# Four lo buffers, activation pairs used in turns, and overwritten TensorE products at the start and between the blocks

## The chip, the cores and the metric

The kernel runs on one core of one Trainium2 chip. The metric is the device time of one execution in microseconds (us), lower is better; the median of the runs is compared. The engines are named as the profile names them: PE is TensorE, with PEld for its weight loads, DVE is VectorE, ACT is ScalarE, POOL is GpSimd, and SP is the engine that issues the DMAs of the weights.

## What is computed

Two different transformer blocks, each two layers deep, run one after the other on one sequence of 256 tokens of width 1024, in fp32. Cut to what matters:

```python
def first_block(x, c, ...):            # 2 layers
    c_act = silu(c)
    for l in range(DEPTH):
        sh1, sc1, gt1, sh2, sc2, gt2 = split(c_act @ w_ada[l] + b_ada[l], 6)
        y = mixer(x * (1 + sc1) + sh1, ...)          # attention and a 31-tap convolution, gated, @ w_out
        x = layer_norm(DN_ALPHA * x + (1 + gt1) * y, ...)
        h = square(relu((x * (1 + sc2) + sh2) @ w_up[l])) @ w_down[l]
        x = layer_norm(DN_ALPHA * x + (1 + gt2) * h, ...)
def second_block(x, ...):              # 2 layers
    for l in range(DEPTH):
        h = rmsnorm(x, ln_mix_g[l])                  # three attentions, gated and merged, @ w_o
        x = x + merged @ w_o[l]
        h = rmsnorm(x, ln_ffn_g[l])
        x = x + (silu(h @ w_ffn_gate[l]) * (h @ w_ffn_up[l])) @ w_ffn_down[l]
    return rmsnorm(x, final_norm_g)
```

So the program is a row of eight stages: mixer and feed-forward of the first block, twice, and the same of the second block, twice.

## The kernel before, in words

**Products.** PE multiplies fp32 operands as sums of three products of a shorter type: each operand is split into a high part (hi) and a remainder (lo), and PE forms hi·hi, hi·lo and lo·hi. Activations are kept as such pairs in SBUF (`u`, and `s`, `mg`, `n_` from `new_fm`).

**Weights.** `fetch()` (L120 to L140) takes the next weight tile of 1 MB: SP's DMA brings it into `raw` (3 buffers), ACT casts it into `whi` (L138, two halves, 4 buffers), DVE subtracts `raw - whi` into `wlo` (L139, two halves, 3 buffers). `w(ahead)` fetches so that one to three tiles are under way before they are used. PE reads `whi` and `wlo` in a few helpers: `ws2` (L175 hi, L177 lo) for the up weights of the feed-forward, `as_` (L206, L207 with lo, L208), and `as_512` (L222, L223 with lo, and L228) for the first piece of a stage. A `wlo` buffer comes free when PE has done its last product from it; until then the DVE subtraction that will fill it again stands and waits, with all that is queued behind it on DVE.

**Order.** PE's order is the order in the code (`manual_schedule` on PE). The orders of DVE and ACT are set by a scheduler at build time, except inside `handover`, where they stand as written too. The scheduler places a cast or a subtraction where it expects its buffers to be free, so the number of buffers changes the order.

**Handovers.** `handover` (L676) joins two stages: the last products of a stage (`out.tail`, with L206 to L208), the normalisation on DVE (`front` and `stats`, for the first block L761 to L778, for the second L841 to L883), eight transposes on PE per half of the tokens (`transposed`, L732), the new hi and lo activations (`finish`, ACT L796 and L801 or L907, DVE L794 and L803 or L905), and the first products of the next stage (`as_512`, L222, L223, L228). The tokens are worked on in two halves of 128, so that each handover has a first and a second set of transposes. There are seven between stages and one at the end. The fourth, between the blocks, is the long one: it has a layer norm and an RMS norm in a row (`ln_rms`).

**Feed-forward of the first block.** Up weights (`ws2`, L175 and L177) and down weights (`add`, L206 to L208) alternate. The up result is evacuated by ACT (L188) and DVE (L189), squared by ACT (L1118, L1119) and split by ACT (L150) and DVE (L151). Between them DVE also does row products for later layers (`ada_dot`, L374) and gates (L419, L421, after the small PE product L418, a 128x128 by 128x256 product in fp32).

**Memory.** Beside `raw`, `whi` and `wlo`, a pool `s8` of four 8 KB buffers holds activations, and `u2` has one pair of 16 KB for `u`.

Of the kernel before, what the change touches and what calls it, by code (L numbers as in the profile page):

```python
# [9 lines left out]
F32 = mybir.dt.float32  # L10
F32R = mybir.dt.float32r
# [5 lines left out]
P = 128  # L17
D = 1024
S = 256
KT = D // P  # L20
# [44 lines left out]
class Net:  # L65
    def __init__(self, ctx, tc, ins, out, stop=None, dump=None):
        self.tc, self.nc, self.i, self.out = tc, tc.nc, ins, out
        self.stop, self.dumps = stop, dump or {}
        self.uid = 0
        self.pools = {}  # L70
        for name, bufs in (("raw", 3), ("whi", 4), ("wlo", 3), ("s8", 4), ("u2", 1), ("s4", 7), ("b4", 2), ("one", 1), ("sm", 3)):
            self.pool(ctx, name, bufs)
        self.pool(ctx, "ps", 8, space=PSUM)
        self.pool(ctx, "dr", 1, space=bass.MemoryType.DRAM)
        self.queue = weight_order(ins)
        self.ready = []
        self.tracks = []
        self.behind = []
        self.ada = {}

# [152 lines left out]
    class Out:  # L233
# [27 lines left out]
        def tail(self, h, *parts):  # L261
            for part in parts:
                for p in self.last:
                    self.emit(p, h, part)


    def rstd(self, v, w):

# [78 lines left out]

    def new_u(self):

        t = self.t("u2", [P, 2, KT, S], F32R)  # L350
        return t[:, 0], t[:, 1], t

    def new_fm(self, n=KT, pool="s8"):
        return self.t(pool, [P, n, S], F32R), self.t(pool, [P, n, S], F32R)

    def par_(self, name, at, n=1):
# [173 lines left out]
    def start(self):  # L530
# [11 lines left out]
        a, n = PC["b_ada"]  # L542
        self.par1 = self.t("one", [P, n], tag="par1")
        nc.vector.tensor_scalar(self.par1, self.par[:, a:a + n], 1.0, None, op0=ALU.add)
        u = self.new_u()
        xT = self.t("s8", [P, KT, S])
        A, B = self.ada_cols(0, 1), self.ada_cols(0, 0)
        ps = [self.ps() for _ in range(8)]
        self.con = self.t("one", [P, NCC], tag="con")
        self.ident = self.con[:, 0:P]  # L550
        a, n = CC["cmask"]
        self.cmask = self.con[:, a:a + n]
        self.x = self.t("one", [P, 2, D], tag="x")
        for k in range(KT):
# [17 lines left out]
            for m in range(4):  # L572
                o = ps[6 + m // 2][:, (m % 2) * S:(m % 2) * S + S]
                b = slice((12 + m) * P, (13 + m) * P)
# [88 lines left out]
    def handover(self, out, ch, nxt=None):  # L663


        res = []
        E = mybir.EngineType
        with self.tc.manual_schedule(engines={E.PE, E.DVE, E.Activation}):
            out.tail(0, *PARTS)
            for _ in ch.front(0):  # L670
                pass
            fill = ch.front(1)
            out.tail(1, *PARTS[:2])
            if ch.ln_rms:
                out.tail(1, PARTS[2])
            ch.stats(0, itertools.islice(fill, 2))  # L676
            ch.transposed(0)
            if not ch.ln_rms:
                out.tail(1, PARTS[2])
            if ch.ln_rms or not ch.u:  # L680
                for _ in fill:
                    pass
            fin = ch.finish(0, fill)
            next(fin)
            g = nxt(ch.u) if nxt else None
            if g:
                next(g)
            for _ in fill:
                pass
            ch.stats(1, fin if ch.ln_rms else ())  # L690
            ch.transposed(1)
            last = [*fin]
            if g:
                res.append(next(g))
            last = [*ch.finish(1)][-1]
            if g:
                res.append(next(g))
        self.behind = [i.ins for i in last]
        self.after = ch.after()
        return res  # L700
# [8 lines left out]
    class Norm:  # L709
# [11 lines left out]
            lo, hi = PARTS[n]  # L721
            return slice(lo, hi), self.acc[h][lo // 512][:, lo % 512:lo % 512 + hi - lo]

        def transposed(self, h):

            net = self.net
            if not self.u:
                return
            ps = [net.ps().rearrange("p (k t) -> p k t", k=4) for _ in range(2)]
            at = self.tr[h] = lambda k, n=1: ps[k // 2 % 2][:, k // 4 * 2 + k % 2:k // 4 * 2 + k % 2 + n, :]  # L730
            for k in range(KT):
                self.nc.tensor.transpose(at(k)[:, 0, :], self.y[h][:, k * P:(k + 1) * P], net.ident)  # L732
# [257 lines left out]
    def mixer1(self, l, u, ps):  # L990
# [58 lines left out]
        def qkf(h):  # L1049
            r = slice(64 * (h % 2), 64 * (h % 2) + 64)  # L1050
            return qT[r, h // 2, :], kT[r, h // 2, :]
        gt = [self.t("s8", [P, KT, S]) for _ in range(2)]

        def gates(b, cs):
            for c in cs:
# [38 lines left out]
        gates(1, [3])  # L1094
        self.finish(ada)
        self.dump(f"hc{l}", hc[0].bitcast(F32))
        mg = self.new_fm()

        def merge(s):
            nc.vector.tensor_add(gt[0][:, s, :], gt[0][:, s, :], gt[1][:, s, :])  # L1100
# [108 lines left out]
    def mixer2(self, l, u, ps):  # L1209
# [1 line left out]
        gq = self.row(i["mla_g"][l])  # L1211

        pcs = [[p for _, p in ps], [p for _, p in self.as_512(u)]]
        n_ = self.new_fm()
        mn = self.mla_norm(pcs, gq, n_)
        next(mn)
        wkr = self.w()
# [4 lines left out]
        p = self.ps()  # L1222
# [43 lines left out]
        for h in range(2):  # L1266
# [3 lines left out]
            for n in range(2):  # L1270
                p = self.ps()
# [5 lines left out]
            kcs.append(kc)  # L1277
        next(gka)
        qTc = self.t("s8x", [P, 8, S])
        kTc = self.t("s8", [P, 8, S])  # L1280
        for src, dst in ((qcs, qTc), (kcs, kTc)):
            for h in range(2):
                tok = slice(h * P, (h + 1) * P)
# [37 lines left out]
            self.dump(f"yb{l}", y[0].bitcast(F32))  # L1321
        ab = self.track(rest(), 22, 62)

        gt = [self.t("s8x" if b == 1 else "s8", [P, KT, S]) for b in range(3)]
        bh = self.small(24, "bgh")
        nc.vector.tensor_scalar(bh, self.par_("b_gate", l * 24, 24), 0.5, None, op0=ALU.mult)
        for b in (2, 0, 1):
            for c in range(4):
                w = self.w()
                for m in range(2):  # L1330
                    k = 2 * c + m
# [1 line left out]
                    nc.scalar.copy(g, p[:, S:])  # L1333
                    nc.vector.tensor_add(g, p[:, :S], g)
                    nc.scalar.activation(g, g, AF.Tanh, scale=0.5, bias=bh[:, b * 8 + k:b * 8 + k + 1])
        mg = self.new_fm()
        for b in (2, 0, 1):
            if b == 1:
                self.finish(ab)
# [156 lines left out]
def build(tc, ins, out, stop=None, dump=None):  # L1496
    with ExitStack() as ctx:
# [5 lines left out]
            net.block1()  # L1503
        if stop is None or stop.startswith("2"):
            with ExitStack() as c2:
                for name, bufs in (("bias", 3), ("s8x", 1)):
                    net.pool(c2, name, bufs)
                net.block2()
        net.dump("x", net.x)
# [148 lines left out]
```

## Time and profile before

| | us |
|---|---|
| median of 3 runs | 1733.07 |
| lowest, highest | 1732.88, 1734.87 |
| the profiled execution | 1733.14 |
| its span in the trace | 1731.2 |
| PE busy in the span | 1661.8 (96%) |
| DVE busy in the span | 1281.8 (74%) |
| ACT busy in the span | 958.8 (55%) |

The profiled execution took 1733.14 us, of which the trace covers 1731.2 us; 1.94 us lie around the span. It is 0.07 us from the median of the runs. The granted TensorE clock was 0.989 of full speed over the span.

A row of a chain or of a timeline reads: start in us from the span's start, duration in us, engine, line, what it does. In square brackets stands how long the engine sat idle before it and whose work ended that idle time. `x8` at the end means that eight like instructions are shown as one row. PE's products are pipelined, so that one product's row overlaps with the next: the time between two starts is what a product costs.

### The profile page before, as it was taken

The numbers are of one execution on the slowest core, as the hardware profiler recorded it, in microseconds if no ns is written. First come the engines' busy times: TensorE is split into PE (matmuls) and PEld (weight loads), VectorE is DVE, ScalarE is ACT, GpSimd is POOL, SyncE is SP. The second block draws the span as 40 slices with busy tenths as digits, with TensorE's granted clock in tenths as the row PEclk, the third lists the DMA queues.
The fourth block names the chain that finished last, engine by engine and source line by source line (L and its number), as shares of the span: only waits on it lengthen the run. The fifth ranks groups of instructions, "written<-read, shape, count | busy, mean of one in ns | idle before, by whom it ended". The sixth has DMA issues, their size and how long they took to land.

```text
span 1731.2 us, 25828 instructions
## 1 busy us (share of the span) xinstructions
PE 1661.8 (96%) x10008; PEld 1436.9 (83%) x10008; DVE 1281.8 (74%) x2497; ACT 958.8 (55%) x1750; POOL 2.6 (0%) x12
## 2 busy tenths in 40 slices
PE   6998999998999999997999999999999999999998
PEld 5887888787888888885988898888889888988887
DVE  7999788578997886557856677766676566876665
ACT  3564375464355375553566754655455677455553
POOL 0000000000000000000000000000000000000000
PEclk9999999999999999998999999999999999999999
DMA  8884568584874466653544444555545444445551
GB/s 337 342 318 173 199 223 316 196 294 176 308 247 182 171 229 233 219 192 140 208 152 150 147 151 179 195 195 195 191 150 203 149 147 146 164 168 198 182 190 72
DMA packets 59974, 347.37 MB, mean 201 GB/s; under 512 B 6558, under 2 KB 10700, under 8 KB 25676
## 3 DMA queue, kind: packets, MB, share of 16 engines
q1 hardware_dynamic: 59852, 345.73, 55.3%
q8 instruction: 78, 1.28, 0.3%
q14 instruction: 44, 0.36, 0.1%
HBM read 344.63 MB, written 2.64 MB: 201 GB/s over the span
## 4 chain that ended last, share of the span: by engine, by line
PE 89%; DVE 7%; DMA 2%; ACT 1%; issue 0%; SPq 0%; DVEq 0%; ACTq 0%
PE ps L175 23%; PE ps L177 12%; PE ps L207 8%; PE ps L206 8%; PE ps L208 8%; PE ps L160 5%; PE ps L161 5%; PE ps L164 4%; PE ps L228 3%; PE ps L222 3%; PE ps L223 2%; DVE wlo L139 2%; PE ps L439 1%; PE ps L332 1%; PE ps L487 1%; PE ps L464 1%
## 5 line engine op out<-in xcount | busy, mean ns | idle before, releaser
L139 DVE TENSOR_TENSOR wlo<-raw,whi 128x1024 fp32r<-128x1024 f32 (+1 forms) x534 | 629.7, 1211 | 206.3 <-PE ps L177 104.0
L138 ACT CAST whi<-raw 128x1024 fp32r<-128x1024 f32 (+1 forms) x534 | 534.1, 1043 | 279.4 <-PE ps L208 80.6
L175 PE MATMUL ps<-u,whi 128*128 128x512 f32 x1728 | 438.9, 396 | 0.0
L175 PEld LDWEIGHTS ps<-u,whi 128*128 128x128 f32 x1728 | 313.9, 188 | 65.3 <-issue 5.7
L206 PE MATMUL ps<-whi,s 128*128 128x512 f32 (+2 forms) x688 | 253.6, 369 | 3.8 <-ACT whi L138 3.8
L207 PE MATMUL ps<-wlo,s 128*128 128x512 f32 (+2 forms) x688 | 253.0, 368 | 0.5 <-DVE wlo L139 0.5
L208 PE MATMUL ps<-whi,s 128*128 128x512 f32 (+2 forms) x688 | 252.3, 367 | 0.0
L177 PEld LDWEIGHTS ps<-u,wlo 128*128 128x128 f32 x1728 | 235.6, 190 | 17.2
L177 PE MATMUL ps<-u,wlo 128*128 128x256 f32 x1728 | 240.7, 282 | 0.0
L206 PEld LDWEIGHTS ps<-whi,s 128*128 128x128 f32 x688 | 130.3, 189 | 23.9 <-ACT whi L138 4.0
L208 PEld LDWEIGHTS ps<-whi,s 128*128 128x128 f32 x688 | 130.0, 189 | 21.0 <-DVE s L151 0.7
L207 PEld LDWEIGHTS ps<-wlo,s 128*128 128x128 f32 x688 | 130.2, 189 | 19.8 <-DVE wlo L139 1.2
L222 PE MATMUL ps<-whi,u 128*128 128x512 f32 x240 | 98.2, 409 | 11.0 <-ACT u L801 10.9
L188 ACT COPY ev<-ps 128x256 f32<-128x256 f32 x136 | 50.2, 369 | 92.1 <-PE ps L177 92.1
L952 DVE SCALAR_TENSOR_TENSOR s<-s,dw,s 128x255 f32<-128x255 f32 (+17 forms) x240 | 96.2, 462 | 0.0
L223 PE MATMUL ps<-wlo,u 128*128 128x512 f32 x240 | 96.0, 400 | 0.0
L160 PE MATMUL ps<-u,whi 128*128 128x256 f32 x352 | 89.4, 292 | 0.2 <-DVE s L941 0.2
L161 PE MATMUL ps<-u,whi 128*128 128x256 f32 x352 | 85.9, 282 | 0.0
L160 PE MATMUL ps<-s,whi 128*128 128x256 f32 x320 | 82.4, 289 | 0.0
L161 PE MATMUL ps<-s,whi 128*128 128x256 f32 x320 | 81.0, 285 | 0.3 <-DVE s L151 0.3
L189 DVE TENSOR_TENSOR ev<-ps,ev 128x256 f32<-128x256 f32 x136 | 56.8, 420 | 28.9 <-ACT ev L188 28.1
L151 DVE TENSOR_TENSOR s<-ev,s 128x256 fp32r<-128x256 f32 (+1 forms) x72 | 39.1, 542 | 48.9 <-PE ps L207 37.7
(263 smaller groups left out, 2123.2 us busy)
## 6 DMA issues: line engine op xcount, KB each, us to landing
raw<-in_w_fgu_dram SPq DMA_DIRECT2D x44, 1024.0 KB, 4.8
raw<-in_w_up_dram SPq DMA_DIRECT2D x32, 1024.0 KB, 5.0
raw<-in_w_down_dram SPq DMA_DIRECT2D x32, 1024.0 KB, 5.6
raw<-in_w_in_dram SPq DMA_DIRECT2D x32, 1024.0 KB, 4.8
ada<-in_w_ada_p_dram SPq DMA_DIRECT2D x48, 512.0 KB, 5.1
raw<-in_w_gate_dram SPq DMA_DIRECT2D x24, 1024.0 KB, 4.8
raw<-in_w_fd_dram SPq DMA_DIRECT2D x22, 1024.0 KB, 4.8
raw<-in_w_in_b_dram SPq DMA_DIRECT2D x18, 1024.0 KB, 6.1
```

The source lines that it names most:

```text
L138: nc.scalar.copy(hi[:, a:b], raw[:, a:b])
L139: nc.vector.tensor_sub(lo[:, a:b], raw[:, a:b], hi[:, a:b].bitcast(F32))
L160: mm(ps, whi[:, b], ahi[:, k, :], start=j == 0, stop=False)
L161: mm(ps, whi[:, b], alo[:, k, :], start=False, stop=False)
L175: mm(p2, whi[:, (blk + k) * P:(blk + k + 1) * P], both[:, :, k, :], start=k == 0, stop=False)
L177: mm(p[:, :S], wlo[:, (blk + k) * P:(blk + k + 1) * P], uhi[:, k, :], start=False, stop=k == KT - 1)
L206: mm(ps, ahi[:, k, tok], whi[:, cols], start=first, stop=False, **grp)
L207: mm(ps, ahi[:, k, tok], wlo[:, cols], start=False, stop=False, **grp)
L208: mm(ps, alo[:, k, tok], whi[:, cols], start=False, stop=last, **grp)
L222: mm(p, ahi[:, k, tok], whi[:, cols], start=k == 0, stop=False)
L223: mm(p, ahi[:, k, tok], wlo[:, cols], start=False, stop=False)
L952: nc.vector.scalar_tensor_tensor(cv[:, ct, d:], hp[:, ct, :S - d], wk, cv[:, ct, d:], op0=ALU.mult, op1=ALU.add)
```

## The change

It has four parts.

- `wlo` has 4 buffers where it had 3.
- The pool `s8` is gone. The pool `u2` holds two tags, `ua` and `ub`, of one 16 KB pair each, and `new_u` takes them in turns. What lived in `s8` (`xT`, the gates `gt`, the merged pair `mg`, the normed pair `n_`) now lives in `ua`, `ub` or the pool `s8x`, which has 2 buffers where it had 1.
- `warm(p, src, n)` writes n products of 128x128 by 128x256 in fp32 into a PSUM tile that the next products overwrite. `start` does 6 of them from `c_row`, which is ready early, ahead of its first product.
- `transposed` does 12 of them from the constants `con` ahead of the first and 8 ahead of the second set of transposes, in the handover between the blocks only.

```diff
-        for name, bufs in (("raw", 3), ("whi", 4), ("wlo", 3), ("s8", 4), ("u2", 1), ("s4", 7), ("b4", 2), ("one", 1), ("sm", 3)):
+        for name, bufs in (("raw", 3), ("whi", 4), ("wlo", 4), ("u2", 1), ("s4", 7), ("b4", 2), ("one", 1), ("sm", 3)):
...
+        self.turn = False
...
+    def warm(self, p, src, n):
+        for _ in range(n):
+            self.nc.tensor.matmul(p[:, :256], src[:, :P], src[:, :256], start=True, stop=True)
...
     def new_u(self):
-        t = self.t("u2", [P, 2, KT, S], F32R)
+        self.turn = not self.turn
+        t = self.pair("ua" if self.turn else "ub", F32R)
         return t[:, 0], t[:, 1], t
-    def new_fm(self, n=KT, pool="s8"):
+    def pair(self, tag, dt=F32):
+        return self.t("u2", [P, 2, KT, S], dt, tag=tag)
+
+    def new_fm(self, n, pool):
...
-        xT = self.t("s8", [P, KT, S])
+        xT = self.pair("ub")[:, 0]
...
         ps = [self.ps() for _ in range(8)]
+        self.warm(ps[0], self.c_row[:, 0:512], 6)
...
-            ch.transposed(0)
+            ch.transposed(0, 12 if ch.ln_rms else 0)
...
-            ch.transposed(1)
+            ch.transposed(1, 8 if ch.ln_rms else 0)
...
-        def transposed(self, h):
+        def transposed(self, h, warm=0):
...
             ps = [net.ps().rearrange("p (k t) -> p k t", k=4) for _ in range(2)]
+            net.warm(ps[0].rearrange("p k t -> p (k t)"), net.con, warm)
...
-        gt = [self.t("s8", [P, KT, S]) for _ in range(2)]
+        gt = self.pair("ub")
+        gt = [gt[:, b] for b in range(2)]
...
-        mg = self.new_fm()
+        mg = self.pair("ua", F32R)
+        mg = mg[:, 0], mg[:, 1]
...
-        n_ = self.new_fm()
+        n_ = self.pair("ub", F32R)
+        n_ = n_[:, 0], n_[:, 1]
...
-        kTc = self.t("s8", [P, 8, S])
+        kTc = self.t("s8x", [P, 8, S])
...
-        gt = [self.t("s8x" if b == 1 else "s8", [P, KT, S]) for b in range(3)]
+        gt = self.pair("ub")
+        gt = [gt[:, 0], self.t("s8x", [P, KT, S]), gt[:, 1]]
...
-                for name, bufs in (("bias", 3), ("s8x", 1)):
+                for name, bufs in (("bias", 3), ("s8x", 2)):
```

The order in which the instructions stand on the engines changes with it. Line numbers of the changed kernel are higher: its L139 and L140 are L138 and L139 of before, L151 and L152 are L150 and L151, L386 is L374, L809 is L794.

DVE in the first handover (mixer to feed-forward), from the residual sum of the second half (L765) on. `wlo` is the lo part of a weight, `x` the residual, `bn` the sums for the norm, `ev` and `u` the activations on their way to PE. Before:

```order
L765 SCALAR_TENSOR_TENSOR x_119<-x_119,ev_2287 128x512
L768 BN_STATS bn_346_2286<-x_119 128x6
L139 TENSOR_TENSOR wlo_2151<-raw_2148,whi_2150 128x1024 x2
L794 TENSOR_SCALAR ev_2284<-ps_2262,pl_a_2161,pl_b_2162 128x128 x2
L768 BN_STATS bn_346_2286<-x_119 128x6
```

The same place in the changed kernel:

```order
L780 SCALAR_TENSOR_TENSOR x_122<-x_122,ev_2288 128x512
L783 BN_STATS bn_344_2287<-x_122 128x6
L809 TENSOR_SCALAR ev_2285<-ps_2263,pl_a_2162,pl_b_2163 128x128 x2
L783 BN_STATS bn_344_2287<-x_122 128x6
L776 TENSOR_TENSOR ev_2298<-ps_2076,G_262_1685 128x256
```

The subtraction for the weight no longer stands between the norm and the activations; it is done before the handover begins. The same pair of subtractions has left the middle of all seven handovers between stages.

ACT in the first feed-forward, around the casts of three weights (`whi_3229`, `whi_3268` and `whi_3329` before; `whi_3230`, `whi_3269` and `whi_3330` in the changed kernel). Before:

```order
L150 CAST s_486_3127<-ev_3083 128x512
L188 COPY ev_3174<-ps_3175 128x256
L188 COPY ev_3174<-ps_3202 128x256
L150 CAST s_501_3223<-ev_3174 128x512
...
L150 CAST s_517_3323<-ev_3274 128x512
L138 CAST whi_3229<-raw_3227 128x1024 x2
L138 CAST whi_3268<-raw_3266 128x1024 x2
L138 CAST whi_3329<-raw_3327 128x1024 x2
```

In the changed kernel:

```order
L151 CAST s_484_3128<-ev_3084 128x512
L139 CAST whi_3230<-raw_3228 128x1024 x2
L189 COPY ev_3175<-ps_3176 128x256
L189 COPY ev_3175<-ps_3203 128x256
...
L151 CAST s_515_3324<-ev_3275 128x512
L139 CAST whi_3269<-raw_3267 128x1024 x2
L139 CAST whi_3330<-raw_3328 128x1024 x2
```

The first of the three casts has moved two up results ahead, the other two stay where they were.

DVE at the same place, from the last evacuation (L189, L190) of the up result on; `ada` is a row product for a later layer, `G` a gate, `s` the split up result. Before:

```order
L189 TENSOR_TENSOR ev_3274<-ps_3302,ev_3274 128x256
L139 TENSOR_TENSOR wlo_3230<-raw_3227,whi_3229 128x1024 x2
L374 ISA ada_3263,ada_515_3298<-ada_3263,c_row_95,par_98 128x1024
L374 ISA ada_515_3298 128x1
L139 TENSOR_TENSOR wlo_3269<-raw_3266,whi_3268 128x1024 x2
L374 ISA ada_3296,ada_515_3298<-ada_3296,c_row_95,par_98 128x1024
L374 ISA ada_515_3298 128x1
L151 TENSOR_TENSOR s_518_3324<-ev_3274,s_517_3323 128x512
L419 TENSOR_TENSOR G_497_3192<-ps_3359,b_447_2881 128x256
```

In the changed kernel:

```order
L190 TENSOR_TENSOR ev_3275<-ps_3303,ev_3275 128x256
L152 TENSOR_TENSOR s_516_3325<-ev_3275,s_515_3324 128x512
L431 TENSOR_TENSOR G_495_3193<-ps_3360,b_445_2882 128x256
L433 TENSOR_SCALAR G_495_3193<-G_495_3193 128x256
L386 ISA ada_3264,ada_513_3299<-ada_3264,c_row_92,par_95 128x1024
L386 ISA ada_513_3299 128x1
L140 TENSOR_TENSOR wlo_3270<-raw_3267,whi_3269 128x1024 x2
```

The subtraction of the first weight is gone from here (it is done earlier), and that of the second, which stood ahead of the split sum `s`, now stands behind it, two gate instructions and a row product.

## Rows read from the trace of the kernel before

**Rows 1.** The page: busy time and share by engine, and the chain that ended last

```profile
PE 1661.8 (96%) x10008; PEld 1436.9 (83%) x10008; DVE 1281.8 (74%) x2497; ACT 958.8 (55%) x1750; POOL 2.6 (0%) x12
...
PE 89%; DVE 7%; DMA 2%; ACT 1%; issue 0%; SPq 0%; DVEq 0%; ACTq 0%
```

**Rows 2.** PE's waits: line, for whom, us in total, times, longest us

```profile
PE ps L732 <- DVE s L883: 18.0, 8, 8.3
...
PE ps L967 <- DVE s L952: 5.8, 1, 5.8
```

**Rows 3.** Timeline of the first handover: start, us, engine, line, [idle before, releaser]

```profile
210.64 2.36 DVE L139 TENSOR_TENSOR wlo<-raw,whi 128x1024 fp32r<-128x1024 f32 x2
...
214.40 0.50 PE L222 MATMUL ps<-whi,u 128*128 128x512 f32 x1 [3.02 <-ACT u L801]
...
219.02 0.54 DVE L778 TENSOR_SCALAR x<-x,mv,r_r 128x512 f32<-128x512 f32 x1
...
220.67 1.04 PE L732 MATMUL ps<-con,x 128*128 128x128 f32 x8
```

**Rows 4.** Two stretches of 2 us: busy time by engine, PEclk, DMA share, GB/s

```profile
216.00:218.00 2.00, 2.00 (x6) 1.58 (x5) 1.79 (x8) 0.41 (x1) 0.00 (x0) 0.50 0.56 234
...
806.00:808.00 2.00, 2.00 (x6) 1.52 (x5) 1.42 (x5) 2.00 (x5) 0.29 (x1) 0.50 0.97 314
```

**Rows 5.** Timeline of PE in the second handover

```profile
411.03 0.50 PE L222 MATMUL ps<-whi,u 128*128 128x512 f32 x1 [3.02 <-ACT u L801]
...
416.34 0.85 PE L732 MATMUL ps<-con,x 128*128 128x128 f32 x6 [0.48 <-DVE x L778]
```

**Rows 6.** The chain of waits in the second handover: start, us, what

```profile
407.27 2.36 DVE wlo L139 x2
```

**Rows 7.** The chain of waits in the fourth handover

```profile
783.44 2.35 DVE wlo L139 x2
```

**Rows 8.** Timeline of PE in the fourth handover

```profile
792.43 1.94 PE L732 MATMUL ps<-con,s 128*128 128x128 f32 x8 [8.28 <-DVE s L883]
...
804.61 1.25 PE L732 MATMUL ps<-con,s 128*128 128x128 f32 x8 [3.44 <-DVE s L883]
```

**Rows 9.** Timeline of the fifth handover

```profile
1073.23 2.36 DVE L139 TENSOR_TENSOR wlo<-raw,whi 128x1024 fp32r<-128x1024 f32 x2 [1.25 <-PE ps L207]
...
1078.65 0.39 PE L223 MATMUL ps<-wlo,u 128*128 128x512 f32 x1
...
1080.79 1.06 PE L732 MATMUL ps<-con,s 128*128 128x128 f32 x8 [1.75 <-DVE s L883]
```

**Rows 10.** Timeline of the first feed-forward, two down weights and the next up weight

```profile
320.26 0.40 PE L206 MATMUL ps<-whi,s 128*128 128x512 f32 x1
...
325.73 0.59 PE L418 MATMUL ps<-b,ones 128*128 128x256 f32 x2
...
325.97 2.19 PE L175 MATMUL ps<-u,whi 128*128 128x512 f32 x8
...
335.08 5.78 ACT L138 CAST whi<-raw 128x1024 fp32r<-128x1024 f32 x6
...
336.18 0.80 PE L206 MATMUL ps<-whi,s 128*128 128x512 f32 x1 [3.84 <-ACT whi L138]
...
338.43 1.28 DVE L374 CUSTOM_DVE_ANT_0 ada<-ada,c_row,par 128x1024 f32<-128x1024 f32 x1
...
344.47 0.69 DVE L151 TENSOR_TENSOR s<-ev,s 128x512 fp32r<-128x512 f32 x1 [1.27 <-PE ps L207]
...
344.74 2.19 PE L175 MATMUL ps<-u,whi 128*128 128x512 f32 x8
...
345.79 2.35 DVE L139 TENSOR_TENSOR wlo<-raw,whi 128x1024 fp32r<-128x1024 f32 x2
...
346.77 1.11 PE L177 MATMUL ps<-u,wlo 128*128 128x256 f32 x8
```

**Rows 11.** Timeline of PE at the start of the program

```profile
26.40 0.50 PE L207 MATMUL ps<-wlo,u 128*128 128x512 f32 x1 [0.50 <-DVE wlo L139]
```

More of the change, by code (lines that the diff above doesn't have):

```diff
@@ L1335, in mixer2 @@
                     nc.scalar.activation(g, g, AF.Tanh, scale=0.5, bias=bh[:, b * 8 + k:b * 8 + k + 1])
-        mg = self.new_fm()
+        mg = self.pair("ua", F32R)
+        mg = mg[:, 0], mg[:, 1]
         for b in (2, 0, 1):
```

## The prediction

> **What bounds the kernel now.** I read the page first. PE is busy 96% of the span, and the chain that ended last is PE for 89% and DVE for 7% [rows 1]. So a gain can come only from the places where the chain leaves PE. The list of PE's waits names them: 18.0 us in eight waits for the norm of the second block (DVE L883), and 5.8 us once for the convolution (DVE L952) [rows 2]. I then followed the chain through each handover and read the timeline beside it. In the first handover it runs over a weight's lo subtraction of 2.36 us that stands between the norm and the activations; PE sits idle 3.02 us until the activations are there [rows 3]. The second has the same subtraction and the same 3.02 us [rows 5, 6], the third is a copy of the second. The fourth, between the blocks, has it too, 2.35 us [rows 7], and there PE waits 8.28 us and 3.44 us [rows 8]. In the fifth it stands ahead of the second half's norm [rows 9]; the sixth and seventh are copies. Last I read the one place outside the handovers where PE waits for a weight: in the first feed-forward it sits idle 3.84 us for a cast [rows 10].
>
> **Part one: the fourth lo buffer, in the handovers.** The subtraction stands there because its buffer is still read by PE: in the fifth handover DVE waits 1.25 us for PE's L207 and then subtracts for 2.36 us [rows 9]. With a fourth buffer it is done in the stage before, where the chain is PE and DVE has room, 74% busy over the span [rows 1]. Its cover is that room; without it, the same 2.36 us would be back in each place.
>
> First handover. PE's first product comes 2.36 us earlier, at 214.40 − 2.36 = 212.04, and the idle time falls from 3.02 to 0.66 us. What is late next is the second set of transposes at 220.67 [rows 3]. In the second handover the same stretch of PE work takes 416.34 − 0.48 − 411.03 = 4.83 us [rows 5]; here it takes 220.67 − 214.40 = 6.27 us, because the granted clock was at its lower level, 1.2 GHz, after the idle time: 0.50 in the stretch from 216 to 218 [rows 4]. With the idle time mostly gone I take the higher level. PE is then through at 212.04 + 4.83 = 216.87. DVE's L778 ends at 219.02 + 0.54 − 2.36 = 217.20. The later of the two starts the transposes: 220.67 − 217.2 ≈ 3.4 us gained, 2.4 if the clock falls all the same.
>
> Second and third. The transposes there already wait for DVE (0.48 us) [rows 5], and PE moves by the same amount as DVE, so all of the 2.36 us counts: 4.7 us.
>
> Fourth. DVE is the chain up to the transposes at 792.43, and again up to those at 804.61 [rows 7, 8], so the 2.35 us count once.
>
> Fifth to seventh. Without the subtraction DVE would let the second transposes start at 1080.79 − 2.36 = 1078.43. PE itself, though, starts its last product of the first half at 1078.65 and needs some 0.23 us for it (two starts of such products lie that far apart), so PE is free at 1078.88. 1080.79 − 1078.88 = 1.9 us each, 5.7 us; 2.36 each, 7.1, is the upper end [rows 9].
>
> A rule of the Trainium skill can be weighed here: "Perfetto Trace Analysis", section Optimization Strategy, says that a gap which repeats on the engine that should be saturated can mean too few buffers for the next tile. By it the whole repeated gap would be the buffer's, and the first three handovers would give 3 × 3.02 = 9.1 us. The trace bears the rule out only in part, 2.36 of 3.02 us, and the first gives 3.4 for a reason of its own; 8.1 us stand in my sum.
>
> **Part one in the first feed-forward.** Before, three casts stand in a row on ACT from 335.08 on, behind the split of an up result, and PE waits 3.84 us for the first of them [rows 10]. A down weight takes 325.73 − 320.26 = 5.47 us when nothing waits, and the small product L418 behind it 325.97 − 325.73 = 0.24 us. From 336.18 − 3.84 = 332.34 the next up weight could so begin at 338.05; it begins at 344.74. So 6.7 us are lost there [rows 10]. In the changed order the first of the casts and its subtraction are done two up results earlier, and this wait goes.
>
> The same reordering adds a wait. The second weight's subtraction now stands behind DVE's L151, which waits for PE's last product of the down weight, and behind the gates and a row product. From L151's start at 344.47 to the end of the gates at 345.79 is 1.32 us, the row product takes 1.28, and one half of the subtraction 2.35 / 2 = 1.18: ready 3.78 us after L151's start. PE needs it 346.77 − 344.47 = 2.30 us after [rows 10]. PE waits 1.5 us. Behind it on DVE stand only a row product and the next weight's subtraction; that one has a whole down weight, 5.47 us, of time. The place gives 6.7 − 1.5 = 5.2 us. The bounds are 6.7 (the operand comes in time) and 2.3: the new wait costs clock as the old one did, whose place lost 6.7 − 3.84 = 2.9 us beside the wait itself [rows 10].
>
> **Part two: pairs in turns, `s8` gone.** It moves operands to other addresses. No instruction is added. A new wait could come where two users share a pair (`gt` and `n_` in `ub`, `mg` in `ua`). Those uses lie a stage apart, and PE's order is the same but for the added products. I take 0, with ±1 us, about the smallest of the stalls above, as bounds.
>
> **Part three: the overwritten products.** A product of this form costs 0.24 us (L418, the same shape) [rows 10]. The 12 take 2.9 us in an idle time of 8.28 − 2.35 = 5.9, the 8 take 1.9 in one of about 3.4 [rows 8]. They fit, so they cost 0. What they can give is clock. After the wait of 3.44 us the granted clock was 0.50, 1.2 GHz, at 806 to 808 [rows 4], and the first-half products before 804.61 are not on the chain, since PE waits for DVE there. I take 0 and keep 2.2 as the upper end: 0.2 for the second transposes, at 1.25 us against 1.06 in the fifth handover [rows 8, 9], 1.0 for the stretch from 806 to 808, and as much again for what lies around that stretch. The 6 at the start can bring the first products forward, but at 26.40 PE waits 0.50 us for a lo part [rows 11]; coming earlier it would wait longer. 0, with −0.3 and +0.5 as bounds.
>
> **The convolution's wait** of 5.8 us [rows 2] stays: DVE's work ahead of it has the same number of instructions in both orders. 0 ± 1.
>
> **The sum.** 3.4 + 4.7 + 2.35 + 5.7 + 5.2 = 21.4 us, against the profiled 1733.14 us, which is its span of 1731.2 and 1.94 around it: **1711.7 us**. The median of the runs lies 0.07 us away, which changes nothing.
>
> **Rivals.**
>
> *The feed-forward gives its gain back.* The new wait on the lo part costs clock as well, and the place gives 2.3, or a second late weight takes that too, and it gives 0: 1714.6 to 1716.9 us. For it: DVE has a new queue ahead of that weight. Against it: the wait, 1.5 us, is half of the one that cost clock in the first handover, and one of 3.02 us in the second cost none (4.83 us of work ran in 4.83).
>
> *The clock holds through the fourth handover.* The added products keep the clock at 2.4 GHz and the first group helps at the start: 2.2 + 0.5 more, 1709.0 us. For it: they fill half of the idle time. Against it: what is left idle ahead of the second transposes is about 3.4 − 1.9 = 1.5 us if the first half's products end where they did, but those end earlier at a higher clock, which leaves about what was idle before. The Trainium skill, "TensorE: Matmul & The Clock Gate", Part 1, says that activity releases the throttle and idleness brings it back; by it this rival would be the likeliest case. In the trace the lower level follows the 3.02 us of the first handover [rows 3, 4] but not the same 3.02 us of the second [rows 5], so the rule does not decide here.
>
> *Slower: lo parts behind a split sum in every feed-forward.* The price of such a place is the 1.5 us worked out above, or 1.5 + 2.9 = 4.4 with the clock. There are 16 up weights in each of the first block's two feed-forwards. If the scheduler put the lo parts of all of them behind L151, and the DMAs arrived later than DVE expects, 32 places at 1.5 cost 48 us. It decides from 21.4 / 1.5 = 15 places on; at 20 the time is 1741 us. Against it: the changed order shows it at one place.
>
> *It doesn't do what it says.* The subtraction leaves the handover in the order, but its raw weight arrives late, so that DVE waits for it at the end of the stage before and the norm starts as late as ever. The handovers then give nothing, the feed-forward 5.2: 1728 us. Against it: the cast and the DMA of those weights were done long before, since in the fifth handover DVE waited for PE's L207, not for them [rows 9].
>
> **How the numbers follow.** The forecast has 0.66, with a range of its own from 1708 to 1715. The feed-forward rival has 0.14, the clock rival 0.10, the one that doesn't do what it says 0.05, the slower one 0.05. A time within 0.2%, 3.5 us, is about what a measurement of this kernel cannot tell from no change; only part of the last two cases ends there. Faster by more than that: 0.66 + 0.14 + 0.10 + 0.03 = 0.93. Same: 0.03. Slower: 0.04. The range goes down to 1705, which takes in the clock rival, the 7.1 and the 6.7 of the upper ends and their small terms, and up to 1720, which takes in the feed-forward rival, the 2.4 of the first handover and the lower ends of parts two and three. It leaves out about 0.15.
>
> **What would show it.** In the changed trace the chain through the seven handovers has no L140 subtraction; PE's first wait in the first three is near 0.7 us; the clock in the first handover stays at 1.0; the second transposes of the fifth to the seventh follow PE's own products; the wait of 3.84 us for a cast is gone, and one of about 1.5 us for a lo part stands some 10 us later in the same stage. The prediction is wrong if lo parts are waited for at more places than that one, if the convolution's wait grows, or if the 12 and the 8 products are still running when the norm is ready.

## The result, and the profile after

| | before | changed |
|---|---|---|
| median us | 1732.97 (4 runs, 1732.07 to 1734.87) | 1709.1 (4 runs, 1708.16 to 1709.7) |
| profiled execution us | 1733.14 | 1708.62 |
| its span us | 1731.2 | 1706.8 |

The ratio is 0.986, with a 95% interval from 0.9843 to 0.9877. The medians lie 23.9 us apart; 21.4 were forecast. Times of one kernel scatter by some us between executions (the kernel before ran from 1730.98 to 1736.24 in 19 runs made for one comparison below), so differences of 1 or 2 us are read from the traces here, place by place.

The page of the changed kernel, busy time and the chain, in the form of [rows 1]:

```profile
PE 1664.3 (98%) x10060; PEld 1440.3 (84%) x10060; DVE 1276.4 (75%) x2497; ACT 955.9 (56%) x1750; POOL 2.6 (0%) x12
...
PE 88%; DVE 7%; DMA 2%; ACT 1%; issue 1%; SPq 0%; ACTq 0%; DVEq 0%
```

PE's waits in the changed kernel (line, for whom, us in total, times, longest):

```profile
PE ps L982 <- DVE s L967: 5.8, 1, 5.8
...
PE ps L747 <- DVE s L898: 4.4, 5, 2.5
```

L747 is L732 of before, L898 is L883, L982 is L967. The wait for the second block's norm was 18.0 us [rows 2] and is 4.4; part of that is real gain and part is filled with overwritten products, which the list counts as work. The wait for the convolution is as it was. New in the list is one wait of 1.3 us for a lo part at L178, shown below.

To see where the time went, the traces are cut at the transposes, because each handover has two sets of them and they are the same work in both kernels. Three first sets of before, in the handovers one, two and five:

```profile
208.89 1.07 PE L732 MATMUL ps<-con,x 128*128 128x128 f32 x8 [1.09 <-DVE x L778]
...
405.52 1.07 PE L732 MATMUL ps<-con,x 128*128 128x128 f32 x8 [1.09 <-DVE x L778]
...
1071.53 1.07 PE L732 MATMUL ps<-con,s 128*128 128x128 f32 x8 [0.35 <-DVE s L883]
```

The changed kernel, first handover; it answers to [rows 3]:

```profile
209.39 1.07 PE L747 MATMUL ps<-con,x 128*128 128x128 f32 x8 [1.09 <-DVE x L793]
...
210.95 0.71 DVE L809 TENSOR_SCALAR ev<-ps,pl_a,pl_b 128x128 f32<-128x128 f32 x2
...
212.42 0.50 PE L223 MATMUL ps<-whi,ub 128*128 128x512 f32 x1 [0.53 <-ACT ub L816]
...
217.76 1.06 PE L747 MATMUL ps<-con,x 128*128 128x128 f32 x8 [0.50 <-DVE x L793]
```

No subtraction stands there, DVE goes straight to the activations, and PE's idle time ahead of its first product is 0.53 us instead of 3.02. From the first to the second set it was 220.67 − 208.89 = 11.78 us and is 217.76 − 209.39 = 8.37: 3.41 us gained.

The second handover of the changed kernel, to be held against [rows 5]:

```profile
397.44 1.07 PE L747 MATMUL ps<-con,x 128*128 128x128 f32 x8 [1.10 <-DVE x L793]
...
405.81 1.06 PE L747 MATMUL ps<-con,x 128*128 128x128 f32 x8 [0.47 <-DVE x L793]
```

From 10.82 us to 8.37: 2.45 us, and the third handover is a copy.

The first feed-forward, to be held against [rows 10]. L430 is L418 of before, L152 is L151, L178 is L177:

```profile
322.86 0.59 PE L430 MATMUL ps<-b,ones 128*128 128x256 f32 x2
...
332.23 3.89 ACT L139 CAST whi<-raw 128x1024 fp32r<-128x1024 f32 x4
...
334.81 0.69 DVE L152 TENSOR_TENSOR s<-ev,s 128x512 fp32r<-128x512 f32 x1 [4.47 <-PE ps L208]
...
337.29 2.35 DVE L140 TENSOR_TENSOR wlo<-raw,whi 128x1024 fp32r<-128x1024 f32 x2
...
338.56 1.22 PE L178 MATMUL ps<-ub,wlo 128*128 128x256 f32 x8 [1.34 <-DVE wlo L140]
```

From the small product to the lo products of the next up weight but one, it was 346.77 − 325.73 = 21.04 us and is 338.56 − 322.86 = 15.70: 5.34 gained, with the new wait of 1.34 us already in it. The row of casts on ACT holds two weights where it held three.

The fourth handover. L271 is the overwritten product, two records for each:

```profile
769.67 5.34 PE L271 MATMUL ps<-con 128*128 128x256 f32 x24
775.87 1.09 PE L747 MATMUL ps<-con,s 128*128 128x128 f32 x8 [0.86 <-DVE s L898]
...
781.96 3.62 PE L271 MATMUL ps<-con 128*128 128x256 f32 x16
788.06 1.09 PE L747 MATMUL ps<-con,s 128*128 128x128 f32 x8 [2.48 <-DVE s L898]
```

And the granted clock behind the second set (last column but two), which was 0.50 some 2 us behind it in the kernel before [rows 4]:

```profile
788.00:790.00 2.00, 1.94 (x13) 1.77 (x14) 0.07 (x2) 1.27 (x5) 0.31 (x1) 1.00 1.04 356
790.00:792.00 2.00, 2.00 (x11) 1.64 (x10) 2.00 (x5) 2.00 (x4) 0.00 (x0) 1.00 0.78 257
```

From the first to the second set it was 804.61 − 792.43 = 12.18 us and is 12.19: DVE sets this, and the clock of PE's products in between changes nothing. From the second set to the first of the fifth handover it was 1071.53 − 804.61 = 266.92 and is 1053.40 − 788.06 = 265.34: 1.6 us gained. All of it lies in the first 6 us behind the second set, where the clock is the difference (1.00 here, 0.50 before).

The fifth handover, to be held against [rows 9]:

```profile
1053.40 1.06 PE L747 MATMUL ps<-con,s 128*128 128x128 f32 x8 [0.35 <-DVE s L898]
...
1055.30 0.76 DVE L920 TENSOR_TENSOR ub<-ps,ub 128x256 fp32r<-128x256 f32 x2 [1.44 <-ACT ub L922]
...
1059.94 0.49 DVE L898 TENSOR_SCALAR s<-s,r_r 128x512 f32<-128x512 f32 x1
...
1060.07 0.39 PE L224 MATMUL ps<-wlo,ub 128*128 128x512 f32 x1
1060.58 1.06 PE L747 MATMUL ps<-con,s 128*128 128x128 f32 x8
```

In the kernel before, the norm ahead of the second set was this row:

```profile
1080.15 0.49 DVE L883 TENSOR_SCALAR s<-s,r_r 128x512 f32<-128x512 f32 x1
```

From 9.26 us to 7.18: 2.1 us. The waits list shows no wait ahead of this second set any more, because PE's last row runs to 1060.46. The starts say otherwise. The next product could have started 0.23 us after 1060.07, at 1060.30. The transposes start at 1060.58, which is 0.15 us after the norm ends (1059.94 + 0.49 = 1060.43), and before it was 0.15 us too (1080.15 + 0.49 = 1080.64, and 1080.79). So DVE still sets the second transposes. The sixth and seventh handovers are copies, with the same 0.15 us.

### The profile page after: what moved, and what is told of

The parts are those of the page before. It is cut to its first block, busy times and chain, and to the rows that moved or that the text cites. A ratio compares the mean times of both kernels' runs of the same rounds, so it can differ in the third digit from the quotient of the medians.

```text
span 1706.8 us, 25931 instructions
## 1 busy us (share of the span) xinstructions
PE 1664.3 (98%) x10060; PEld 1440.3 (84%) x10060; DVE 1276.4 (75%) x2497; ACT 955.9 (56%) x1750; POOL 2.6 (0%) x12
## 4 chain that ended last, share of the span: by engine, by line
PE 88%; DVE 7%; DMA 2%; ACT 1%; issue 1%; SPq 0%; ACTq 0%; DVEq 0%
PE ps L176 23%; PE ps L178 12%; PE ps L207 7%; PE ps L208 7%; PE ps L209 7%; PE ps L161 5%; PE ps L162 5%; PE ps L165 5%; PE ps L223 3%; PE ps L229 3%; PE ps L224 3%; DMA raw<-in_w_in_a_dram 2%; PE ps L451 1%; PE ps L339 1%; DVE wlo L140 1%; PE ps L499 1%
## 5 line engine op out<-in xcount | busy, mean ns | idle before, releaser
L140 DVE TENSOR_TENSOR wlo<-raw,whi 128x1024 fp32r<-128x1024 f32 (+1 forms) x534 | 631.9, 1212 | 258.9 <-ACT whi L139 256.0
L139 ACT CAST whi<-raw 128x1024 fp32r<-128x1024 f32 (+1 forms) x534 | 535.1, 1043 | 285.5 <-PE ps L209 75.1
L176 PE MATMUL ps<-ub,whi 128*128 128x512 f32 x1088 | 273.2, 393 | 0.0
L176 PEld LDWEIGHTS ps<-ub,whi 128*128 128x128 f32 x1088 | 198.6, 188 | 37.5
L207 PE MATMUL ps<-whi,s 128*128 128x512 f32 (+1 forms) x464 | 174.6, 376 | 0.0
L208 PE MATMUL ps<-wlo,s 128*128 128x512 f32 (+1 forms) x464 | 174.3, 376 | 0.0
L209 PE MATMUL ps<-whi,s 128*128 128x512 f32 (+1 forms) x464 | 173.9, 375 | 0.0
L176 PE MATMUL ps<-ua,whi 128*128 128x512 f32 x640 | 165.7, 401 | 0.0
L178 PEld LDWEIGHTS ps<-ub,wlo 128*128 128x128 f32 x1088 | 148.3, 190 | 12.4 <-DVE wlo L140 1.8
L178 PE MATMUL ps<-ub,wlo 128*128 128x256 f32 x1088 | 151.8, 282 | 1.3 <-DVE wlo L140 1.3
L176 PEld LDWEIGHTS ps<-ua,whi 128*128 128x128 f32 x640 | 115.4, 188 | 27.8 <-issue 5.7
L207 PEld LDWEIGHTS ps<-whi,s 128*128 128x128 f32 x464 | 87.5, 189 | 15.2 <-issue 0.6
L208 PEld LDWEIGHTS ps<-wlo,s 128*128 128x128 f32 x464 | 87.5, 189 | 14.2
L967 DVE SCALAR_TENSOR_TENSOR s<-s,dw,s 128x255 f32<-128x255 f32 (+14 forms) x240 | 96.3, 463 | 0.0
L189 ACT COPY ev<-ps 128x256 f32<-128x256 f32 x136 | 50.1, 368 | 81.3 <-PE ps L178 81.2
L178 PEld LDWEIGHTS ps<-ua,wlo 128*128 128x128 f32 x640 | 87.2, 190 | 6.5
L161 PE MATMUL ps<-ua,whi 128*128 128x256 f32 x352 | 89.3, 292 | 1.0 <-DVE s L956 1.0
L178 PE MATMUL ps<-ua,wlo 128*128 128x256 f32 x640 | 89.0, 282 | 0.0
L162 PE MATMUL ps<-ua,whi 128*128 128x256 f32 x352 | 85.9, 282 | 0.0
```

The source lines that it names most:

```text
L139: nc.scalar.copy(hi[:, a:b], raw[:, a:b])
L140: nc.vector.tensor_sub(lo[:, a:b], raw[:, a:b], hi[:, a:b].bitcast(F32))
L161: mm(ps, whi[:, b], ahi[:, k, :], start=j == 0, stop=False)
L162: mm(ps, whi[:, b], alo[:, k, :], start=False, stop=False)
L176: mm(p2, whi[:, (blk + k) * P:(blk + k + 1) * P], both[:, :, k, :], start=k == 0, stop=False)
L178: mm(p[:, :S], wlo[:, (blk + k) * P:(blk + k + 1) * P], uhi[:, k, :], start=False, stop=k == KT - 1)
```

## The experiments

Two theories of where the gain comes from were set against each other: the fourth lo buffer, or the pairs in turns, which could free the new activations from the old pair. A third question was what the overwritten products are worth, and at which of the three places.

**Three lo buffers, all else changed.**

```diff
-        for name, bufs in (..., ("wlo", 4), ...):
+        for name, bufs in (..., ("wlo", 3), ...):
```

> The changed kernel with three lo buffers again; pairs in turns and overwritten products are kept. Theory (the fourth lo buffer makes nearly all of the gain): the subtraction is back in the seven handovers and the cast is late again in the first feed-forward; about 1731.5 us, 1.5 less than before for the clock in the fourth handover. Rival (pairs in turns free the handovers, since the new activations need no longer wait for the old pair): it stays below 1716 us.

Measured: 1735.06 us, ratio to before 1.0002 (0.999 to 1.0014). Its waits for the activations in the handovers and for the late cast are back:

```profile
PE ps L223 <- ACT ub L816: 7.3, 4, 3.0
...
PE ps L207 <- ACT whi L139: 4.9, 3, 3.8
```

The gain is gone with the one buffer. The 1.5 us that the products should have left don't show in the times, and the interval is too wide to deny them. In the trace they are there: from the second set of the fourth handover to the first of the fifth it is 1073.56 − 808.20 = 265.36 us, as in the changed kernel. This execution lost them again elsewhere. Its first feed-forward, from set to set, takes 187.41 us instead of 184.85 (2.6 more; the cause was not followed), and its second and third handovers take 11.62 and 11.78 us instead of 10.82 (1.8 more). For the handovers the clock tells why: after the same idle time of 3.02 us it was at 0.50 in all three first handovers of this execution, where in the profiled one of before it was only in the first.

```profile
216.00:218.00 2.00, 2.00 (x7) 1.52 (x6) 1.88 (x7) 1.05 (x3) 0.00 (x0) 0.50 0.90 381
...
414.00:416.00 2.00, 1.69 (x4) 1.40 (x5) 1.97 (x6) 1.97 (x6) 0.00 (x0) 0.50 0.80 279
...
606.00:608.00 2.00, 2.00 (x6) 1.61 (x5) 1.82 (x8) 0.74 (x2) 0.00 (x0) 0.50 0.81 340
```

**Pairs in turns alone.** Three lo buffers and no overwritten product.

```diff
-        for name, bufs in (..., ("wlo", 4), ...):
+        for name, bufs in (..., ("wlo", 3), ...):
...
-        self.warm(ps[0], self.c_row[:, 0:512], 6)
...
-            ch.transposed(0, 12 if ch.ln_rms else 0)
+            ch.transposed(0)
...
-            ch.transposed(1, 8 if ch.ln_rms else 0)
+            ch.transposed(1)
```

> Three lo buffers and no overwritten products: of the change only the pairs in turns and the second buffer of s8x are left. Theory: nothing, 1733 us within 1.5. Rival (pairs free the handovers): below 1718 us.

Measured: 1733.33 us, ratio 1.0001 (0.9991 to 1.0012). The wait for the late cast is there:

```profile
PE ps L207 <- ACT whi L139: 5.2, 2, 3.8
```

The pairs give nothing by themselves. They make room: the kernel before with a fourth lo buffer and nothing else would leave 4.25 KB of each partition for the pool of the gate rows, which takes 12, so that this step could not be timed alone. It is shown, then, that the gain needs the fourth buffer and that the pairs without it give nothing; what the buffer would give without the pairs is not shown.

**No overwritten products**, four lo buffers and pairs kept.

```diff
-        self.warm(ps[0], self.c_row[:, 0:512], 6)
...
-            ch.transposed(0, 12 if ch.ln_rms else 0)
+            ch.transposed(0)
...
-            ch.transposed(1, 8 if ch.ln_rms else 0)
+            ch.transposed(1)
```

> The changed kernel without the 26 overwritten products; four lo buffers and pairs are kept. Theory: the products only hold the clock behind the second transposes of the fourth handover, 1.5 us, and give nothing at the start; 1710.6 us, with a granted clock of 0.5 for some 3 us there. Rival (the products are worth more, by the start or by both halves of that handover): 1713 us or more. Second rival (they are worth nothing, the clock would have held without them): 1709.1 us, clock 1.0.

Measured: 1711.37 us, ratio 0.9868 (0.9853 to 0.9884). By ratio it is 0.0008 or 1.4 us behind the changed kernel, within both intervals. Lines behind the start of the program are one lower in this kernel and the next two (L746 for L747). Both sets of transposes of the fourth handover ran at half clock, and so did what follows:

```profile
777.88 1.94 PE L746 MATMUL ps<-con,s 128*128 128x128 f32 x8 [6.13 <-DVE s L897]
...
790.08 1.94 PE L746 MATMUL ps<-con,s 128*128 128x128 f32 x8 [4.77 <-DVE s L897]
...
1057.66 1.06 PE L746 MATMUL ps<-con,s 128*128 128x128 f32 x8 [0.34 <-DVE s L897]
```

```profile
790.00:792.00 2.00, 1.92 (x9) 1.95 (x10) 0.00 (x0) 0.54 (x2) 0.00 (x0) 0.50 1.08 364
```

From the second set to the first of the fifth handover it is 1057.66 − 790.08 = 267.58 us, 2.2 more than in the changed kernel.

**Only the 12, only the 8.** Two kernels without the 6 at the start; each keeps one group in the fourth handover.

```diff
-            ch.transposed(1, 8 if ch.ln_rms else 0)
+            ch.transposed(1)
```

> The changed kernel with the 12 overwritten products ahead of the first transposes of the fourth handover only; the 6 at the start and the 8 ahead of the second transposes are left out. Theory (each idle stretch needs its own products, as the kernel without any had the clock at 0.50 after both): clock 1.0 through the first half's products, then 0.50 for some 4 us behind the second transposes; the handover is 1.5 to 2.5 us longer than with both. Rival (what the clock loses behind the second transposes comes from the first half having run slowly): clock 1.0 in both, nothing lost.

```diff
-            ch.transposed(0, 12 if ch.ln_rms else 0)
+            ch.transposed(0)
```

> The changed kernel with the 8 overwritten products ahead of the second transposes only. Theory (the first half's products lie off the chain, which is DVE there): clock at 0.50 behind the first transposes, 1.0 behind the second; the handover is as short as with both groups, within 0.5 us. Rival: the first half, at half clock, ends so late that the 8 products delay the second transposes; 1 us or more is lost.

Measured: 1710.93 us, ratio 0.987 (0.9853 to 0.9886) with the 12, and 1707.97 us, ratio 0.9851 (0.9834 to 0.9867) with the 8. With the 12 alone the second set is slow, and the stretch behind it:

```profile
787.94 1.94 PE L746 MATMUL ps<-con,s 128*128 128x128 f32 x8 [6.06 <-DVE s L897]
...
1055.63 1.06 PE L746 MATMUL ps<-con,s 128*128 128x128 f32 x8 [0.34 <-DVE s L897]
```

```profile
790.00:792.00 2.00, 2.00 (x6) 1.52 (x6) 1.40 (x5) 2.00 (x5) 0.30 (x1) 0.50 0.60 199
```

With the 8 alone the first set is slow and the second is not:

```profile
775.22 1.94 PE L746 MATMUL ps<-con,s 128*128 128x128 f32 x8 [6.13 <-DVE s L897]
...
783.75 3.62 PE L271 MATMUL ps<-con 128*128 128x256 f32 x16
...
787.32 1.09 PE L746 MATMUL ps<-con,s 128*128 128x128 f32 x8
...
1052.66 1.07 PE L746 MATMUL ps<-con,s 128*128 128x128 f32 x8 [0.34 <-DVE s L897]
```

```profile
788.00:790.00 2.00, 2.00 (x12) 1.70 (x11) 0.80 (x3) 1.76 (x5) 0.31 (x1) 1.00 1.08 360
```

From the first to the second set it is 12.28 us with the 12 and 12.10 with the 8, against 12.19 with both. From the second set to the first of the fifth handover it is 1055.63 − 787.94 = 267.69 us with the 12 and 1052.66 − 787.32 = 265.34 with the 8, which is what the changed kernel has. So the first theory of each run held. The 12 do nothing for the time. The 8 do all of it, and they end just when the norm is ready, with no idle time left. The times of the two kernels say the same (1710.53 to 1712.87 and 1707.94 to 1708.57 us, three runs each), though the intervals of the ratios overlap. Neither kernel has the 6 at the start, and the one with the 8 is as fast as the changed kernel without them.

**Products in the wait for the convolution.** A place that the change leaves alone: PE waits 5.8 us for DVE, and behind it ran at half clock.

```diff
             for ct in range(4):
+                if l == 0 and h == 0 and ct == 2:
+                    self.warm(p[:, 2 * P:], self.con, 20)
                 nc.tensor.transpose(p[:, ct * P:(ct + 1) * P], ...)
```

> The changed kernel with 20 more overwritten products in the idle stretch of 5.8 us in which PE waits for the convolution of the first mixer. Theory (the products behind that wait, at half clock for 6.8 us, are on the chain): the clock holds at 1.0 there and about 3 us are gained, 1706 us. Rival (DVE, busy all through this stretch, is what ends last behind the convolution): the clock holds but less than 1 us is gained.

Measured: 1711.57 us, ratio 0.9873 (0.9856 to 0.9889). No gain: the products themselves ended late. (L984 here is L982 of the changed kernel.)

```profile
143.32 8.80 PE L271 MATMUL ps<-con 128*128 128x256 f32 x40
...
151.96 0.82 PE L984 MATMUL ps<-con,s 128*128 128x128 f32 x6
```

They cover 8.80 us where 5.8 were free, so that the transposes came 151.96 − 149.22 = 2.7 us later than in the changed kernel:

```profile
149.22 1.69 PE L982 MATMUL ps<-con,s 128*128 128x128 f32 x6 [5.82 <-DVE s L967]
```

The clock held at 1.00, and by the products at 164 us the delay was made up (the same row starts at 164.22, and at 164.17 in the changed kernel). The price of one is 8.80 / 20 = 0.44 us. So the same was tried with 12. (The next expectation gives this delay as 3.05 us; the rows give 2.7.)

> The changed kernel with 12 instead of 20 overwritten products in the wait for the convolution of the first mixer. One product takes 0.44 us in the traces (20 took 8.80), so 12 take 5.3 us and fit in the 5.8 us. Theory: the clock holds at 1.0 and nothing is late; about 2.9 us less than the changed kernel, which is what the run with 20 won back after it had come 3.05 us late. Rival (with PE faster, DVE is late behind the convolution): less than 1 us.

Measured: 1707.93 us, ratio 0.9862 (0.9846 to 0.9878), not to be told from the changed kernel.

```profile
143.30 5.35 PE L271 MATMUL ps<-con 128*128 128x256 f32 x24
149.27 1.13 PE L984 MATMUL ps<-con,s 128*128 128x128 f32 x6 [0.63 <-DVE s L967]
...
158.75 0.63 PE L339 MATMUL ps<-con,ev 128*128 128x128 f32 x4 [0.56 <-DVE ev L989]
```

The products fit, nothing is late, and the transposes are faster. Some of what PE wins it loses at L339, where it now waits 0.56 us for DVE, which has been busy all the while. In its trace about 1.5 us are left of the gain (the first transposes of the first handover come at 207.83 instead of 209.39): between the theory and the rival, and too small for the runs to show.

**The kernel before, once more.**

> The kernel before, once more, for a second look at its trace. Theory (after the idle time of 3.02 us in the first three handovers the clock falls in some executions and not in others): another set of the three is at 0.50 than the first alone. Rival (the place decides): the first alone again. And the waits for the ada_p weights between 470 and 480 us, 1.1 us, are there again if they belong to the order of before; if they were chance, they are gone.

Measured: 1734.04 us. Its clock in the first three handovers:

```profile
216.00:218.00 2.00, 2.00 (x6) 1.61 (x5) 1.93 (x6) 1.32 (x4) 0.00 (x0) 0.50 0.99 418
...
414.00:416.00 2.00, 2.00 (x10) 1.67 (x9) 1.76 (x7) 0.04 (x1) 0.00 (x0) 1.00 0.39 160
...
602.00:604.00 2.00, 2.00 (x6) 1.52 (x6) 1.97 (x6) 1.66 (x4) 0.00 (x0) 0.50 0.88 365
```

The first and the third fell, the second did not: the execution decides, not the place. PE's waits for the ada_p weights between 470 and 480 us are gone in this execution, and in those of the two kernels with three lo buffers, so the 1.3 us by which the profiled execution of the changed kernel was shorter there are chance.

## Why the prediction was right, step by step

| step | forecast | measured in the traces |
|---|---|---|
| first handover | 3.4 | 3.4 |
| second and third | 4.7 | 4.9 |
| fourth, up to the second transposes | 2.35 | 2.2 |
| fifth to seventh | 5.7 | 6.2 |
| first feed-forward | 5.2 | 5.3 |
| clock behind the fourth handover | 0 (up to 2.2) | 1.6 |
| products at the start | 0 | no gain |
| waits for ada_p weights | not named | 1.3, chance |
| pairs in turns | 0 | 0 |

The fourth's 2.2 is the difference between the two traces from the second transposes of the third handover (607.32 before, 593.00 in the changed kernel) to the first of the fourth: 185.11 − 182.87. The rest of the 24.4 us between the two spans, about −0.5, lies ahead of the first handover, whose first transposes come at 209.39 instead of 208.89. It arises behind the convolution: from its transposes (149.49 before, 149.22 now) on, the clock stays low for longer, at 0.50 and then 0.80 from 152 to 156, where it was 0.65 and then 1.00. Whether the change or chance does this is open; the two executions of the kernel before start that handover at 208.89 and 209.84, and the three kernels with four lo buffers and without the 6 products between 208.66 and 211.37. The 6 show no gain beside that.

**The handovers.** The first four went as worked out. In the first the clock stayed up, so the second transposes wait for DVE, as forecast (the forecast's own figures give 3.47, which it wrote as 3.4). In the fifth to seventh the number came near by luck. The forecast took PE's own end as the later one, 1.9 us, and DVE as 2.36 us earlier. Both moved otherwise. PE's first half got shorter: its L229 (L228 before) had waited for the lo activations, which come behind the subtraction on DVE. PE could have started the second set 1060.30 − 1053.40 = 6.90 us after the first, 2.36 us sooner than before. DVE gained only 2.1 us: before, it waited 1.25 us for PE and then subtracted for 2.36 [rows 9]; now it waits 1.44 us for ACT's hi activations (L922). That wait, hidden by the subtraction before, is what the forecast left out. So DVE is late, 0.3 us behind PE, and the sign that the prediction named, second transposes that follow PE's own products, did not come.

**The first feed-forward** went as worked out to 0.1 us, the new wait included: 1.5 forecast, 1.34 measured. The rival in which it costs clock did not come: the clock is 1.00 from 336 to 344.

**The clock behind the fourth handover** is the term that was sized wrong. The prediction took 0, on the ground that about the same idle time would be left ahead of the second transposes. What failed there is the price of a product. It was read as 0.24 us from two starts, L418 and the next L175 [rows 10]; the traces show 5.34 / 12 = 0.44. The trace starts the rows of the up weight too early there. The time comes out one step later, as two up weights of before show, the first behind an L418 and the second not:

```profile
347.72 2.00 PE L175 MATMUL ps<-u,whi 128*128 128x512 f32 x8
349.56 1.12 PE L177 MATMUL ps<-u,wlo 128*128 128x256 f32 x8
```

Without the small product, eight L175 take 349.56 − 347.72 = 1.84 us; with it, 346.77 − 344.74 = 2.03 [rows 10]. 0.24 + 0.19 = 0.43 is the whole price. The Trainium skill, "FP8 and Floating Point Precision", section TensorE Precision Notes, counts four passes for a true fp32 product. Products of 256 columns start 0.12 us apart in the handovers (L207 and L208), so an estimate by that page is 4 × 0.12 = 0.48 us, near the 0.44 measured. With the true price the 8 fill 3.6 us of the 6.06 that stand there without them, the idle time left is 2.48 us in this trace, and the clock held. At 0.24 us some 4.1 would have been left, more than the 3.44 behind which the clock fell before. No run tried that; the one with the 8 alone, which leaves no idle time, held the clock too. So the rival in which the clock holds came true where it mattered, by 1.6 of its 2.7 us; the start gave nothing. In the runs with one group each the clock was up behind the group that was there (1.00 from 776 to 786 with the 12, and from 782 to 796 with the 8) and down behind the one that was not (0.50 from 788 to 792, and from 776 to 780). This bears out the rule that the prediction cites beside this rival from the Trainium skill, "TensorE: Matmul & The Clock Gate", Part 1, that activity releases the throttle. That the 12 don't matter was right in the prediction: PE's first half is off the chain.

**What the prediction feared and did not come:** lo parts late at many places (one new, of 1.34 us; four others, 3.0 us together, lie in the first 47 us, where before has three with 1.4), a raw weight that is late, a longer wait for the convolution (5.8 us in both).

## What to carry to other kernels

A subtraction that waits for its buffer costs about its length wherever the chain runs over its engine, not where the engine is busiest: 2.45 us for one of 2.36 in the second handover, but 2.1 in the fifth, where the next wait stood right behind it. One more buffer moved it to a stage with room, and the pairs in turns made that buffer fit; alone they gave nothing. Where a scheduler places work by the buffers, look at what else it moves: here it cured one late weight and made another late. In this kernel overwritten products were worth their place only ahead of work that is on the chain, and their number has to come from a measured price, since too many of them are a wait of their own. And where a list shows no wait, the starts of the rows and the end of the work ahead still tell which engine is late.

## What the runs showed of the hardware that was not expected

The clock's fall after one and the same idle time is not settled by the program. With three lo buffers PE waited 3.02 us in each of the first three handovers. In four executions (two of the kernel before, the three-buffer kernel, the pairs alone) the clock fell to 0.50 or near it in 8 of these 12 places: in the first handover each time, in the second once, in the third three times. With the idle time at some 0.5 us it stayed at 1.00 in the first three handovers of the changed kernel and of all five others with four lo buffers. A shorter idle time so gives more than its length, and what more is differs between executions.

A product of two fp32 operands, 128x128 by 128x256, took 0.44 us, though the trace of before let two starts stand 0.24 us apart.
